# Second mixer: the values of the linear attention are projected ahead of the LRU's gate

## Chip, cores and metric

One core of a Trainium2 chip. The metric is the device time of one execution in microseconds (us); before the change the median of 3 runs is 734.24 us (732.68 to 735.36).

## What is computed

Two transformer blocks in float32 on 256 tokens of width 1024. The change lies in the mixer of the second block, which joins three branches:

```
z = einsum('bsd,de->bse', rms_norm(x, norm_mix), w_in)
a_x, a_y, b_q, b_f, b_i, b_g, c_q, c_k, c_v = split(z)
ya = rglru_group(a_x, a_y, ...)      # h = scan(conv(a_x)); h * gelu(a_y)
yb = hgrn2_group(b_q, b_f, b_i, b_g) # chunked recurrence with values b_i; rms_norm(o) * silu(b_g)
yc = moba_group(c_q, c_k, c_v)       # attention
y = concat([rms_norm(ya), yb, rms_norm(yc)])
x = x + einsum('bse,ed->bsd', y, w_out)
```

`a_y` gates the LRU's scan; `b_i` are the values of the linear attention (the recurrence); `b_g` gates its normed output.

## The kernel before, in words

Weights are streamed. `Weights` holds a list of chunks (1 MB each for this projection, 256 columns of the output); a DMA on SP brings a chunk into one of two `raw` buffers, and each half chunk (a unit) is split into a high part (`whi`, ScalarE, line 130) and the rest (`wlo`, VectorE, line 131). `blocks` takes two units of a chunk one after the other; for each it makes one output block of 128 columns by 256 tokens in PSUM (`mm`): 8 steps of k with 3 products each (`whi` with `ah`, `whi` with `al`, `wlo` with `ah`), 24 products. All products are issued by the helper at line 260, transposes at line 256; small operations go through helpers at lines 214 (two tensors), 233 (scalar, tensor, tensor), 228 and 229 (tensor, scalars), 236 and 239 (ScalarE).

`mixer2` walks over `self.c_in2`, which pairs the names of the table `ORDER2` with the chunks of `w_in_2`; `laid_out` packs that matrix in the table's order, so the table alone says in which order the 12 chunks come. For each block that is ready, `mixer2` does what its name asks: for `a_y` the gelu by tanh, in `gyz` and `gy` (product with `rb`, square, `gy`, tanh, `gy`); for `b_i` a copy `vt`, transposes and a scaling into `hv`; for `b_g` a product `hgz`, a tanh and `hgg`. After the chunk `a_x` the generator `lru` is started, after `b_i` the recurrence `hg` is finished and its tail `hg_out` started, after `c_v` half of the attention's heads (`moba`). Generators are advanced one piece after each block (`bg.step`). A scheduler then lays the instructions of each engine in its order; the engines run their queues in that order and wait on semaphores.

`lru` needs both blocks of `a_y`: after its scans (`xc`, line 1204) it multiplies by `gy`, squares into `lt`, sums the two halves, lets TensorE sum over the partitions (`ones`,`lt`), makes the reciprocal root on VectorE (`ncv`, `ncw`, `ncr`, eight small operations), broadcasts it by TensorE (`ident`,`ncr`), and writes the normed result split into `mab`. `moba` ends in the same norm over its sum of squares `ycs` and writes `mc`. `hg_out` multiplies the recurrence's matrices `attT` and `attX` with `hv`, squares (`hee`), sums per head (`cst`,`hee`), makes its root (`hn`), waits until `b_g` has been gated, and writes the other half of `mab`.

After the loop `bg.finish(lr, *mo)` completes `lru` and `moba`; then the output projection begins with its four first blocks on `lru`'s half of `mab` and on `mc`, and takes the recurrence's half last.

Of the kernel before, what the change touches and what calls it, by code (L numbers as in the profile page):

```python
# [1710 lines left out]
def tile_two_blocks(ctx, tc, I, out, dbg=None, auto=True):  # L1711
    if not auto:
# [2 lines left out]


ORDER2 = (("b_f", 768), ("b_q", 512), ("c_q", 1536), ("c_k", 2048), ("c_v", 2560), ("c_q", 1792),
          ("c_k", 2304), ("c_v", 2816), ("a_x", 0), ("a_y", 256), ("b_i", 1024), ("b_g", 1280))


def _spans(widths):
# [108 lines left out]
```

## Time and profile before

| | us |
|---|---|
| median of 3 runs | 734.24 |
| the profiled execution's own time | 730.46 |
| its span, first to last instruction | 728.7 |
| TensorE busy (products) | 703.0, 96% |
| VectorE busy | 559.0, 77% |
| ScalarE busy | 436.5, 60% |
| mean granted TensorE clock | 0.995 |

A row of the profile gives the line, the engine, the operation, what it writes and from what, and the count. A float32 product appears as two records for one instruction, so a count of 8 can be four instructions. Products overlap, so busy time says little; what counts is when the next one starts.

### The profile page before, as it was taken

To read this page: it belongs to the slowest core of one execution; us is meant where nothing else is said; L and a number is where in the kernel's file an instruction comes from. 1 tells how busy PE (TensorE), PEld (TensorE's weight loads), DVE (VectorE), ACT (ScalarE), POOL (GpSimd) and SP (SyncE) were. 2 spreads that over 40 slices of the span, in tenths; PEclk is the share of its full clock that TensorE was granted. 3 is DMA by queue.
4 is the path that set the end of the run, shared out by engine and by line. 5 is a ranking of instruction groups with operands and counts; after the bars stand their busy time and mean duration, and the time that the engine had idled before them with its cause. 6 is when DMAs were issued, how large, how long until landed. Compare 5 with 4: busy or idle time off the path is not lost.

```text
span 728.7 us, 13820 instructions
## 1 busy us (share of the span) xinstructions
PE 703.0 (96%) x5442; PEld 664.3 (91%) x5442; DVE 559.0 (77%) x1240; ACT 436.5 (60%) x807; POOL 24.3 (3%) x74
## 2 busy tenths in 40 slices
PE   8998998999999999999999998999899999999996
PEld 5887897989999999999999998898799999988895
DVE  8997787987989987887656598997777777744533
ACT  7489558655566655555455486769467666643421
POOL 5020000000001000000000200000000000000000
PEclk9999999999999999999999999999999999999999
DMA  7552303236555655455556545332237665565521
GB/s 256 201 185 107 117 2 116 66 109 207 184 189 203 212 193 175 174 174 181 179 177 215 183 167 174 116 115 69 107 116 239 205 220 176 188 215 177 182 107 58
DMA packets 18225, 117.25 MB, mean 161 GB/s; under 512 B 2160, under 2 KB 2416, under 8 KB 5360
## 3 DMA queue, kind: packets, MB, share of 16 engines
q1 hardware_dynamic: 17136, 113.55, 45.8%
q0 software_dynamic: 448, 2.16, 0.8%
q8 instruction: 43, 0.70, 0.4%
q10 hardware_dynamic: 576, 0.65, 0.3%
q14 instruction: 22, 0.18, 0.1%
HBM read 115.30 MB, written 1.05 MB: 160 GB/s over the span
## 4 chain that ended last, share of the span: by engine, by line
PE 79%; DVE 11%; ACT 6%; DMA 2%; issue 1%; SPq 0%; DVEq 0%; ACTq 0%
PE mm L260 71%; PE ps L260 6%; DVE wlo L131 2%; PE ps L256 1%; ACT whi L130 1%; DVE s5w L214 1%; DMA cst<-in_cst_dram 1%; ACT s5tz L239 1%; DVE s5bc L214 1%; DMA raw<-in_w_up_dram 1%; ACT us L239 1%; DVE s5x L214 1%; PE pso L260 1%; ACT msc L236 1%; DVE s5an L233 1%
## 5 line engine op out<-in xcount | busy, mean ns | idle before, releaser
L130 ACT ACTIVATE whi<-raw 128x1024 fp32r<-128x1024 f32 (+1 forms) x206 | 215.4, 1051 | 200.5 <-PE mm L260 172.7
L131 DVE TENSOR_TENSOR wlo<-raw,whi 128x1024 fp32r<-128x1024 f32 (+1 forms) x206 | 249.8, 1214 | 108.2 <-ACT whi L130 106.8
L260 PE MATMUL mm<-ah,whi 128*128 128x258 f32 (+2 forms) x992 | 281.8, 284 | 0.5 <-DVE a L214 0.5
L260 PE MATMUL mm<-al,whi 128*128 128x258 f32 (+2 forms) x992 | 280.6, 283 | 0.0
L260 PE MATMUL mm<-ah,wlo 128*128 128x258 f32 (+2 forms) x992 | 280.3, 283 | 0.0
L260 PEld LDWEIGHTS mm<-ah,whi 128*128 128x128 f32 x992 | 187.8, 189 | 2.2 <-issue 1.0
L260 PEld LDWEIGHTS mm<-al,whi 128*128 128x128 f32 x992 | 187.8, 189 | 1.8 <-issue 1.1
L260 PEld LDWEIGHTS mm<-ah,wlo 128*128 128x128 f32 x992 | 187.9, 189 | 0.5 <-issue 0.4
L260 PE MATMUL mm<-wlo,f2h 128*128 128x256 f32 (+1 forms) x160 | 55.6, 348 | 0.0
L260 PE MATMUL mm<-whi,f2h 128*128 128x256 f32 (+1 forms) x160 | 55.5, 347 | 0.0
L260 PE MATMUL mm<-whi,f2l 128*128 128x256 f32 (+1 forms) x160 | 55.5, 347 | 0.0
L260 PE MATMUL mm<-fh,whi 128*128 128x256 f32 x176 | 48.6, 276 | 0.0
L260 PE MATMUL mm<-fl,whi 128*128 128x256 f32 x176 | 48.6, 276 | 0.0
L260 PE MATMUL mm<-fh,wlo 128*128 128x256 f32 x176 | 48.6, 276 | 0.0
L260 PEld LDWEIGHTS mm<-whi,f2h 128*128 128x128 f32 x160 | 30.3, 189 | 3.9
L260 PEld LDWEIGHTS mm<-wlo,f2h 128*128 128x128 f32 x160 | 30.3, 189 | 3.8
L260 PEld LDWEIGHTS mm<-whi,f2l 128*128 128x128 f32 x160 | 30.3, 189 | 3.8
L260 PEld LDWEIGHTS mm<-fh,whi 128*128 128x128 f32 x176 | 33.0, 188 | 0.0
L260 PEld LDWEIGHTS mm<-fl,whi 128*128 128x128 f32 x176 | 33.0, 188 | 0.0
L260 PEld LDWEIGHTS mm<-fh,wlo 128*128 128x128 f32 x176 | 33.0, 188 | 0.0
L260 PE MATMUL mm<-hT,whi 128*128 128x272 f32 (+1 forms) x128 | 29.3, 389 | 0.7 <-ACT ah L239 0.7
L260 PEld LDWEIGHTS mm<-hT,whi 128*128 128x128 f32 x128 | 23.8, 190 | 5.9 <-ACT ah L239 1.5
(411 smaller groups left out, 1092.9 us busy)
## 6 DMA issues: line engine op xcount, KB each, us to landing
raw<-in_w_ff_dram SPq DMA_DIRECT2D x32, 1024.0 KB, 4.8
raw<-in_w_in_dram SPq DMA_DIRECT2D x24, 1024.0 KB, 4.8
raw<-in_w_up_dram SPq DMA_DIRECT2D x22, 1024.0 KB, 4.8
raw<-in_w_down_dram SPq DMA_DIRECT2D x8, 1024.0 KB, 4.8
whi<-in_w_in_dram SPq DMA_DIRECT2D x8, 512.0 KB, 5.4
raw<-in_w_o_dram SPq DMA_DIRECT2D x4, 1024.0 KB, 4.7
raw<-in_w_out_dram SPq DMA_DIRECT2D x4, 1024.0 KB, 4.8
raw<-in_w_down_dram SPq DMA_DIRECT2D x4, 768.0 KB, 4.4
```

Of the source, the lines that this page charges most:

```text
L130: b.A.activation(out=hi[:, 0:m], in_=raw, func=AF.Copy)
L131: b.V.tensor_tensor(out=lo[:, 0:m], in0=raw, in1=hi[:, 0:m].bitcast(F32), op=ALU.subtract)
L214: return self.V.tensor_tensor(out=o, in0=a, in1=b, op=op)
L233: return self.V.scalar_tensor_tensor(out=o, in0=a, scalar=s, in1=b, op0=op0, op1=op1)
L236: return self.A.activation(out=o, in_=i, func=f, **k)
L239: return self.A.activation(out=o, in_=i, func=AF.Copy)
L256: return self.PE.transpose(out=o, in_=i, identity=self.ident[0:k, 0:k])
L260: return self.PE.matmul(out=o, lhsT=l, rhs=r, start=start, stop=stop)
```

## The change

Two chunks trade places in the table: `b_i` comes before `a_y`. Nothing else is edited; the packing of the weights follows the table.

```
 ORDER2 = (("b_f", 768), ("b_q", 512), ("c_q", 1536), ("c_k", 2048), ("c_v", 2560), ("c_q", 1792),
-          ("c_k", 2304), ("c_v", 2816), ("a_x", 0), ("a_y", 256), ("b_i", 1024), ("b_g", 1280))
+          ("c_k", 2304), ("c_v", 2816), ("a_x", 0), ("b_i", 1024), ("a_y", 256), ("b_g", 1280))
```

How this moves the instructions is seen at three places. The first is TensorE at the end of the loop, from the last block product of `b_g` to the first product of the output projection. Before:

```order
L260 MATMUL mm<-ah,wlo 128x256
L260 MATMUL ps<-ident,ncr 128x128 x2
L260 MATMUL ps<-attT,hv 64x128 x2
L260 MATMUL ps<-attX,hv 64x128 x2
L260 MATMUL ps<-attT,hv 64x128 x4
L260 MATMUL ps<-attX,hv 64x128 x2
L260 MATMUL ps<-attT,hv 64x128 x2
L260 MATMUL ps<-ones,ycs 128x1 x2
L260 MATMUL mm<-mab,whi 128x256 x4
```

After the change, the same place:

```order
L260 MATMUL mm<-ah,wlo 128x256
L260 MATMUL ps<-ones,lt 128x1 x2
L260 MATMUL ps<-ident,ncr 128x128 x2
L256 MATMUL ps<-ident,hn 4x128 x2
L260 MATMUL ps<-ones,ycs 128x1 x2
L260 MATMUL mm<-mab,whi 128x256 x4
```

And after the change where the blocks of `a_y` end and those of `b_g` begin (its first product is the third row here):

```order
L260 MATMUL pso<-mwt,cvn 64x256 x2
L260 MATMUL pso<-mwt,cvn 64x128 x2
L260 MATMUL mm<-ah,whi 128x256
L260 MATMUL ps<-cst,hee 128x2 x4
L260 MATMUL mm<-al,whi 128x256
L260 MATMUL mm<-ah,wlo 128x256
```

The twelve products with `hv` have left the end (they stand between the two blocks of `a_y`), `cst`,`hee` has moved ahead of `b_g`'s blocks, and `ones`,`lt`, which stood 19 block products before the loop's end, stands behind the last.

The second place is the gelu of `a_y`'s second block, on VectorE and ScalarE. VectorE before, from `gyz` to the last `gy`:

```order
L214 TENSOR_TENSOR gyz<-mm,rb_5197 128x256
L1430 ISA msc,msm<-ps,cst 128x128
L1430 ISA msm 128x1
L1430 ISA msc,msm<-ps,cst 128x256
L1430 ISA msm 128x1
L131 TENSOR_TENSOR wlo<-raw,whi 128x1024
L233 SCALAR_TENSOR_TENSOR gy<-gy,gyz 128x256
L228 TENSOR_SCALAR msm<-msm 128x2
L1445 COPY mwt<-ps 128x384
L233 SCALAR_TENSOR_TENSOR lrd<-lrd,lt 128x512
L233 SCALAR_TENSOR_TENSOR gy<-gy,gyz 128x256
```

VectorE after the change, from the first scan on:

```order
L1204 SCALAR_TENSOR_TENSOR xc<-lrd,lth 128x256
L233 SCALAR_TENSOR_TENSOR gy<-gy,gyz 128x256
L1204 SCALAR_TENSOR_TENSOR xc<-lrd,lth 128x256
L214 TENSOR_TENSOR gyz<-mm,rb_5197 128x256
L229 TENSOR_SCALAR hn<-ps 128x8
L229 TENSOR_SCALAR hn<-hn 128x8
L214 TENSOR_TENSOR hn<-hn 128x8
L233 SCALAR_TENSOR_TENSOR hn<-hn 128x8 x2
L131 TENSOR_TENSOR wlo<-raw,whi 128x1024
L233 SCALAR_TENSOR_TENSOR gy<-gy,gyz 128x256
L214 TENSOR_TENSOR hn<-hn 128x8
L131 TENSOR_TENSOR wlo<-raw,whi 128x1024
```

ScalarE there after the change, from the exchange of its table of functions to the second tanh:

```order
L236 ACT_TABLE_LOAD
L236 ACTIVATE gy<-gy 128x256
L236 ACTIVATE hee<-ps 128x512
L239 ACTIVATE hls<-ps 128x512
L130 ACTIVATE whi<-raw 128x1024
L236 ACTIVATE gy<-gyz 128x256
L130 ACTIVATE whi<-raw 128x1024
L239 ACTIVATE yc<-pso 128x256
L130 ACTIVATE whi<-raw 128x1024
L236 ACTIVATE gy<-gy 128x256
```

The last `gy` stood six operations ahead of the scans; now the second block's begins behind both scans, with the splits of two units in its way on either engine.

The third place is VectorE from the last `gy` to the norm `ncv` of the LRU. Before, from the scans on:

```order
L1204 SCALAR_TENSOR_TENSOR xc<-lrd,lth 128x256 x2
L1445 COPY mwt<-ps 128x384
L131 TENSOR_TENSOR wlo<-raw,whi 128x1024
L214 TENSOR_TENSOR xc<-xc,gy 128x512
L131 TENSOR_TENSOR wlo<-raw,whi 128x1024
L214 TENSOR_TENSOR lt<-lt 128x256
L214 TENSOR_TENSOR hgz<-mm,rb_5197 128x256
L229 TENSOR_SCALAR ncv<-ps 128x2
```

After the change, from the last `gy` on:

```order
L233 SCALAR_TENSOR_TENSOR gy<-gy,gyz 128x256
L233 SCALAR_TENSOR_TENSOR hn<-hn 128x8
L214 TENSOR_TENSOR ycs<-ycs,sqc 128x256
L214 TENSOR_TENSOR xc<-xc,gy 128x512
L233 SCALAR_TENSOR_TENSOR hgg<-hgg,hgz 128x256
L131 TENSOR_TENSOR wlo<-raw,whi 128x1024
L214 TENSOR_TENSOR lt<-lt 128x256
L214 TENSOR_TENSOR hgz<-mm,rb_5197 128x256
L229 TENSOR_SCALAR ncv<-ps 128x2
```

Before, the product of `xc` with `gy` followed the scans; now it follows the last `gy`.

## Rows read from the trace of the kernel before

**Rows 1.** The page: busy time by engine, and the chain that ended last.

```profile
PE 703.0 (96%) x5442; PEld 664.3 (91%) x5442; DVE 559.0 (77%) x1240; ACT 436.5 (60%) x807; POOL 24.3 (3%) x74
...
PE 79%; DVE 11%; ACT 6%; DMA 2%; issue 1%; SPq 0%; DVEq 0%; ACTq 0%
```

**Rows 2.** Busy time by stretch: length, engines, granted clock, DMA share, GB/s.

```profile
512.00:521.00 9.00, 6.35 (x62) 5.80 (x62) 7.01 (x28) 4.24 (x10) 0.00 (x0) 0.97 0.38 129
521.00:535.00 14.00, 13.98 (x106) 13.61 (x107) 8.67 (x25) 6.82 (x14) 0.00 (x0) 0.89 0.00 1
```

**Rows 3.** TensorE's waits, 412 to 570 us: total us, times, longest.

```profile
PE ps L260 <- DVE ncr L233: 1.4, 2, 0.9
PE mm L260 <- ACT mc L239: 1.4, 1, 1.4
```

**Rows 4.** The chain that ended last, in order of time: start, us, what.

```profile
421.48 15.72 PE mm L260 x136
...
511.87 1.07 ACT whi L130
```

**Rows 5.** Timeline, gelu of the second block of `a_y`: start, us, engine, line, operation.

```profile
494.74 0.43 DVE L214 TENSOR_TENSOR gyz<-mm,rb 128x256 f32<-128x256 f32 x1 [1.03 <-PE mm L260]
...
496.03 0.41 ACT L236 ACTIVATE gy<-gyz 128x256 f32<-128x256 f32 x1
...
498.04 0.41 ACT L236 ACTIVATE gy<-gy 128x256 f32<-128x256 f32 x1
...
498.79 0.42 DVE L233 SCALAR_TENSOR_TENSOR gy<-gy,gyz 128x256 f32<-128x256 f32 x1
```

**Rows 6.** Timeline, the LRU branch from its scans to the output projection.

```profile
503.57 1.27 DVE L1204 TENSOR_TENSOR_SCAN xc<-lrd,lth 128x256 f32<-128x256 f32 x2
...
506.35 0.68 DVE L214 TENSOR_TENSOR xc<-xc,gy 128x512 f32<-128x512 f32 x1
...
509.64 0.16 DVE L229 TENSOR_SCALAR ncv<-ps 128x2 f32<-128x2 f32 x1 [0.48 <-PE ps L260]
...
512.88 0.71 PE L260 MATMUL ps<-ident,ncr 128*128 128x128 f32 x4 [0.93 <-DVE ncr L233]
```

**Rows 7.** Timeline of TensorE, the small products around the loop's end.

```profile
505.35 0.86 PE L260 MATMUL pso<-mwt,cvn 128*64 128x256 f32 x6
...
509.10 0.50 PE L260 MATMUL ps<-ones,lt 128*128 128x1 f32 x4
...
513.52 0.44 PE L260 MATMUL ps<-attT,hv 128*64 128x128 f32 x4
...
514.98 0.61 PE L260 MATMUL ps<-ones,ycs 128*128 128x1 f32 x4
515.45 0.72 PE L260 MATMUL mm<-mab,whi 128*128 128x256 f32 x4
...
517.48 0.28 PE L260 MATMUL mm<-mab,wlo 128*128 128x256 f32 x1
518.19 0.68 PE L260 MATMUL ps<-ident,ncr 128*128 128x128 f32 x4 [0.43 <-DVE ncr L233]
518.71 0.95 PE L260 MATMUL ps<-cst,hee 128*128 128x2 f32 x8
521.02 1.22 PE L260 MATMUL mm<-mc,whi 128*128 128x256 f32 x4 [1.36 <-ACT mc L239]
```

**Rows 8.** Busy time in two single microseconds behind the holes (columns as rows 2).

```profile
522.00:523.00 1.00, 1.00 (x7) 1.00 (x6) 1.00 (x5) 0.53 (x2) 0.00 (x0) 0.50 0.00 0
524.00:525.00 1.00, 1.00 (x9) 0.80 (x8) 0.00 (x0) 0.37 (x1) 0.00 (x0) 1.00 0.06 16
```

**Rows 9.** Timeline of ScalarE, the exchange of its table of functions.

```profile
499.62 1.28 ACT L236 ACT_TABLE_LOAD   x1
...
500.91 0.63 ACT L236 ACTIVATE lth<-lt 128x512 f32<-128x512 f32 x1
```

## The prediction

> **What bounds the kernel now.** I read the page first. TensorE is busy for 96% of the span and holds 79% of the chain that ended last, so a change elsewhere pays only where TensorE stands still [rows 1]. Next come the stretches around the edit: from 512 to 521 us TensorE is busy for 6.35 of 9 us, and from 521 to 535 us it is busy throughout but at a mean granted clock of 0.89 [rows 2]. TensorE's waits between 412 and 570 us name what it stood for: twice the reciprocal root `ncr` of a norm (1.4 us in all), and once the split normed attention output `mc` (1.4 us) [rows 3]. With the issue gaps around them these are three holes: 511.8 to 512.88, 517.6 to 518.19, and 519.66 to 521.02 us [rows 4, 7]. The end of the first is the LRU branch's norm, that of the other two the attention's. Until 511.8 us TensorE runs block products almost without a hole (the first weight slot of the last chunk comes free at 511.87 us); 136 of them took 15.72 us, so one costs 0.116 us, and a chunk of 48 costs 5.5 us [rows 4].
>
> **What the change removes and adds.** Nothing: the same blocks, the same DMAs, the same count of instructions. Two chunks trade places in the stream; the weights are packed in the same table's order, so SP's and POOL's queues are unchanged. Only the order on TensorE, VectorE and ScalarE moves.
>
> **What comes earlier.** The values `b_i` are ready one chunk sooner, so the recurrence's 12 output products (`attT`, `attX`, from 513.52 to 514.98, 1.46 us [rows 7]) and the four `cst`,`hee` products of its norm (0.95 us [rows 7]) now run before the last chunk `b_g`, where before they stood behind it. That is 2.4 us of TensorE work taken out from behind the last chunk. In return `ones`,`lt` (0.50 us [rows 7]) moves from the middle of that chunk to behind it. The last block therefore ends near 511.8 + 1.46 + 0.95 - 0.50 = 513.7 us.
>
> **What comes later.** The gate chunk `a_y` is now the last but one. Its end, counted back from 513.7 us: 48 block products of `b_g` (5.5 us), `hee` (0.95) and the last `pso` group (0.86, [rows 7]) come after it, so its second block ends near 506.4 us. From there one chain runs over VectorE and ScalarE to TensorE:
> 1. The order puts the second `gyz` behind the second scan on VectorE; two scans took 1.27 us [rows 6], one is 0.6. Bounds 0 and 1.3 us; I take 0.6, one scan: `gyz` at 507.0.
> 2. The gate itself. Before, the second block took from 494.74 to 499.21 us, 4.5 us [rows 5], of which the four operations are 1.7 and the rest queueing. Now two `whi` and a `yc` stand on ScalarE between square and tanh, and two `wlo` with four small `hn` operations on VectorE. Bounds 4.5 (as before) and 5.5 (one more `whi`, 1.07 us [rows 4]); I take 5.0: 512.0 us.
> 3. One `ycs` addition stands ahead of `xc`x`gy`: 0.3 us. Then `xc`x`gy` to the norm's first operation `ncv`, 506.35 to 509.64 before, 3.3 us [rows 6]: 515.6 us. There is one `wlo` in that piece now and two before, but `hgg` and a `whi` have joined, so I keep 3.3.
> 4. `ncv` to the product with `ncr`, 509.64 to 512.88 before, 3.2 us [rows 6], again with a `wlo` and three short operations between: 518.8 us.
>
> Before, the same product started at 512.88 us and TensorE had waited 1.1 us for it. Now it starts 5.9 us later; TensorE has been out of block products since 513.7 us and waits some 4.6 us, with only `ones`,`lt` between. What is queued behind it on TensorE is every output projection.
>
> **Behind that product.** The 2.4 us of recurrence work is already done: -2.4. But it was also the cover of the next wait: from the `ncr` product to the first `mab` product passed 2.57 us (512.88 to 515.45 [rows 6, 7]), filled with these products. Now `ncr`, two transposes and `ones`,`ycs` fill about 1.3 of them: +1.3. The attention's norm, formerly bare (0.6 and 1.4 us [rows 3, 7]), now has the `mab` products and the gated recurrence beside it; I give back 1.6 of these 2.0 us, bounds 1.1 and 2.0.
>
> **Clock.** At 522 to 523 us the clock is 0.50, the 1.2 GHz level, after TensorE had been idle for 1.4 us and thinly used before; at 524 to 525 us it is full again [rows 8]. Seven products in that microsecond against nine in the later one, over about 3 us from 521 us on, cost at least 0.7 us; by the block's 0.116 us doubled, 1.5 us. The new wait is longer, so I expect the fall to come earlier and to cost about the same: 0, bounds -1.5 (no fall) and +1.5 (a second one).
>
> **Sum.** +5.9 - 2.4 + 1.3 - 1.6 + 0 = **+3.2 us**. The profiled execution took 730.46 us, 0.5% under the median of 734.24; the sum is a difference inside one stage, so I put it on the median: 737.4 us (733.7 on that execution). Low ends together (0, 4.5, gain 2.0, clock -1.5): about 0; high ends (1.3, 5.5, gain 1.1, clock +1.5): about +6.5.
>
> **Rivals.**
> - *Covered chain, no change* (0.20): the gate chain runs nearer to its four operations' 1.7 us than to 4.5, say 3.0 us, since the tail has VectorE less full. Then the shift is 3.9 instead of 5.9 and the sum +1.2: 735.4 us. Against: VectorE was busy 7.01 of 9 us there [rows 2], with wide splits in order.
> - *The recurrence's tail was what held the end* (0.07), faster: if the LRU norm's product came no later than 514.8 us, as close behind the last block as before (1.1 us), the shift would be 1.9 instead of 5.9, all of the attention's 2.0 us of waits would go and the half clock's 1.5 with them: +1.9 - 2.4 + 1.3 - 2.0 - 1.5 = -2.7, 731.5 us. It decides at `gy` ready by 514.8 - 3.2 - 3.3 - 0.3 = 508.0 us, 1.6 us after its block's end; the four operations alone take 1.7 [rows 5].
> - *The reload lands on the chain* (0.04): the square root's table of functions is loaded at 499.62 us [rows 9] and exchanged back later; the change moves that exchange ahead of the first block's tanh, and VectorE holds the first block's last `gy` between the two scans, with the second block's `gyz` behind them. Where the exchange ends last there, its 1.29 us (499.62 to 500.91 [rows 9]) come on top: 738.7 us. Against: the first block has 2.8 us of block products as a lead. The Trainium skill (ScalarE: Activation LUTs, What ACT_TABLE_LOAD costs) gives 1.28 us for the load and a drain of about 1.38 besides; by it this case would be 740.1 us. The trace disagrees about the drain: the next operation starts 0.01 us after the load's end.
> - *The clock falls and stays* (0.06): the wait before `ncr` is followed by thin work and a second wait. If a second stretch at 1.2 GHz follows, block products at twice 0.116 us lose another 1.5 us: 738.9 us, and 740.2 with the exchange. For it: the half clock followed a shorter hole [rows 8]. The Trainium skill (TensorE: Matmul & The Clock Gate, What's actually happening) lets the clock go by how busy TensorE has lately been; the trace agrees with one fall here, and no row of before shows two.
>
> **How the numbers follow.** My forecast, a bare LRU chain, has 0.63. 0.3% of 734.24 is 2.2 us, about what a measurement of this kernel can tell from no change: the band is 732.0 to 736.4. The forecast, the exchange and the clock lie above it but for the forecast's low tail (0.04), which with the covered chain makes 0.24; faster is 0.07, slower 0.69. The range goes from 734.6, inside the covered case, to 740.2, the end of the clock case.
>
> **What would show it.** Right: TensorE's longest wait of the second mixer is on `ncr`, 3 to 5 us, right behind the last block products; `xc`x`gy` starts some 6 us later than 506.35; the waits on `mc` shrink below 0.5 us; everything before `a_x` is the same. Wrong: `xc`x`gy` within 2 us of its old time, or TensorE's wait on `ncr` staying near 1 us, or a new wait ahead of the recurrence's output products.

## The result and the profile after

| | before | after |
|---|---|---|
| median of 17 runs, us | 731.76 | 736.75 |
| lowest to highest, us | 728.97 to 735.36 | 734.63 to 739.70 |
| the profiled execution's own time, us | 730.46 | 734.94 |
| its span, us | 728.7 | 733.2 |
| mean granted TensorE clock | 0.995 | 0.992 |

The changed kernel is slower: ratio 1.0068, 95% interval 1.0053 to 1.0083, which is 5.0 us. The trace after is of a run on the quick side: its 734.94 us is the second lowest of the 17, and its mean granted clock the highest of them (their median is 0.988). The page, against [rows 1]: the busy times are the same but for the clock, and in the chain that ended last VectorE has 13% where it had 11.

```profile
PE 705.3 (96%) x5442; PEld 667.0 (91%) x5442; DVE 559.0 (76%) x1240; ACT 436.6 (60%) x807; POOL 24.2 (3%) x74
...
PE 78%; DVE 13%; ACT 6%; issue 2%; DMA 1%; SPq 0%; DVEq 0%
```

The same two stretches as [rows 2], then four single microseconds against [rows 8] (columns as in rows 2):

```profile
512.00:521.00 9.00, 3.10 (x17) 2.62 (x15) 6.01 (x19) 2.75 (x5) 0.00 (x0) 0.73 0.57 208
521.00:535.00 14.00, 13.23 (x91) 13.05 (x92) 7.42 (x25) 4.12 (x10) 0.00 (x0) 0.81 0.02 8
...
515.00:516.00 1.00, 0.00 (x0) 0.00 (x0) 1.00 (x6) 0.00 (x1) 0.00 (x0) 1.00 0.00 0
516.00:517.00 1.00, 0.00 (x0) 0.00 (x0) 1.00 (x2) 0.00 (x0) 0.00 (x0) 0.57 0.00 0
...
526.00:527.00 1.00, 1.00 (x8) 0.92 (x7) 0.56 (x2) 0.49 (x2) 0.00 (x0) 0.81 0.00 0
527.00:528.00 1.00, 1.00 (x9) 0.99 (x9) 1.00 (x4) 0.96 (x3) 0.00 (x0) 1.00 0.00 0
```

From 512 to 521 us TensorE is busy for 3.10 us where it was 6.35. The clock falls to its 1.2 GHz level within 516 to 517 us, while TensorE is idle, and is full again within 526 to 527 us; the nine microseconds between read 0.50. A mean of 0.57 is 0.86 us at half clock and 0.81 is 0.38, so the stretch lasts 0.86 + 9 + 0.38 = 10.24 us. The single microseconds of before give 3.41 in the same way, from 520.5 us on.

TensorE's waits from 412 to 575 us, against [rows 3] (total us, times, longest):

```profile
PE ps L260 <- DVE ncr L233: 3.5, 1, 3.5
PE ps L260 <- DVE lt L214: 2.1, 1, 2.1
PE ps L260 <- DVE qzs L228: 1.7, 1, 1.7
...
PE mm L260 <- ACT mab L239: 1.1, 1, 1.1
```

The wait on the attention's scaled queries `qzs` lies far ahead of the edit and is no part of the loss: it was there before, 1.8 us, the longest wait of the window, though [rows 3] don't show it. Both waits on the attention's norm are gone, `mc` and the second `ncr`. In their place TensorE waits 2.1 us for `lt`, the input of the LRU norm, 3.5 us for that norm, and 1.1 us for the first `mab`. The rows answering to [rows 6, 7], in order of time:

```profile
506.16 0.40 DVE L214 TENSOR_TENSOR gyz<-mm,rb 128x256 f32<-128x256 f32 x1
...
511.62 0.69 DVE L214 TENSOR_TENSOR xc<-xc,gy 128x512 f32<-128x512 f32 x1
...
514.98 0.16 DVE L229 TENSOR_SCALAR ncv<-ps 128x2 f32<-128x2 f32 x1 [0.42 <-PE ps L260]
...
518.41 1.19 PE L260 MATMUL ps<-ident,ncr 128*128 128x128 f32 x4 [3.47 <-DVE ncr L233]
```

The chain that ended last, from the second gate block to the norm's product (start, us, what), in place of TensorE's block products:

```profile
507.74 1.22 DVE wlo L131
508.96 0.33 DVE gy L233
509.29 0.08 DVE hn L214
509.37 1.13 DVE wlo L131
510.50 0.07 DVE hn L233
510.58 0.34 DVE hgz L214
510.92 0.38 DVE gy L233
...
512.64 1.14 DVE wlo L131
513.79 0.44 DVE lt L214
...
516.01 1.14 DVE wlo L131
...
518.10 0.17 DVE ncr L233
518.28 0.14 issue
518.41 1.19 PE ps L260 x4
```

Of the 12.25 us from `gyz` (506.16) to the product (518.41), four `wlo` hold 1.22 + 1.13 + 1.14 + 1.14 = 4.63. None of them belongs to the LRU branch. They split weights of the mixer's output projection and stand in VectorE's queue between the chain's own steps. Ahead of the first line shown, the chain comes from TensorE's `cst`,`hee` through five small `hn` operations, which also stand in that queue, behind `gyz`.

**Where the 5 us lie.** The second mixer's stage can be measured within one execution, from the first `ident`,`msc` product after 480 us to the last `mc`,`wlo` product. After:

```profile
484.02 0.33 PE L256 MATMUL ps<-ident,msc 128*128 128x128 f32 x1 [0.35 <-ACT msc L236]
...
547.73 0.28 PE L260 MATMUL mm<-mc,wlo 128*128 128x256 f32 x1
```

That is 63.71 us. Before, the same two products start at 485.04 and 543.32: 58.28 us. The stage is 5.43 us longer. TensorE's holes in it are the waits with the issue gaps: 2.27 + 3.63 + 1.27 = 7.17 us after, 1.10 + 0.60 + 1.53 = 3.23 us before, a difference of 3.94. The clock: after, TensorE was idle for 2.27 us (516.14 to 518.41) and 1.27 us of the 10.24, so 6.7 us of work ran at half speed, which cost half of that, 3.35 us. Before, 2.9 us of work ran so, from 521.02 us to the end of the stretch near 523.94, and cost 1.46. That is 1.9 us more. Holes and clock together make 5.8 us against the 5.43 measured.

That the two come so close is partly chance, for one thing more differs. At full clock, and with TensorE busy throughout, the products near the stage's end start 0.1178 us apart after and 0.1133 us before. Ten microseconds of each, after first (columns as in [rows 2]):

```profile
536.00:546.00 10.00, 10.00 (x87) 10.00 (x87) 10.00 (x20) 6.88 (x14) 0.00 (x0) 1.00 0.34 111
532.00:542.00 10.00, 10.00 (x91) 10.00 (x90) 10.00 (x20) 6.98 (x15) 0.00 (x0) 1.00 0.31 107
```

Over the 21 us from the clock's return to the stage's end that is another 0.8 us (an estimate: 21 x 0.0045 / 0.1178), so the rest of the stage must have been quicker after; that was not taken apart. The two profiled executions as a whole differ by 4.5 us, since the one after reached the stage 1.02 us earlier.

### The profile page after: what moved, and what is told of

It reads as the page before. It is cut to its first block, busy times and chain, and to the rows that moved or that the text cites. A ratio compares the mean times of both kernels' runs of the same rounds, so it can differ in the third digit from the quotient of the medians.

```text
span 733.2 us, 13820 instructions
## 1 busy us (share of the span) xinstructions
PE 705.3 (96%) x5442; PEld 667.0 (91%) x5442; DVE 559.0 (76%) x1240; ACT 436.6 (60%) x807; POOL 24.2 (3%) x74
## 4 chain that ended last, share of the span: by engine, by line
PE 78%; DVE 13%; ACT 6%; issue 2%; DMA 1%; SPq 0%; DVEq 0%
PE mm L260 69%; PE ps L260 7%; DVE wlo L131 3%; PE ps L256 1%; DVE s5w L214 1%; ACT s5tz L239 1%; DMA cst<-in_cst_dram 1%; DVE s5bc L214 1%; ACT whi L130 1%; ACT us L239 1%; DVE s5x L214 1%; PE pso L260 1%; DVE s5an L233 1%; ACT u L239 1%; DVE qzs L214 0%
## 6 DMA issues: line engine op xcount, KB each, us to landing
whi<-in_w_in_dram SPq DMA_DIRECT2D x8, 512.0 KB, 5.6
```

## The experiments

Three theories were to be told apart. **A**: the gate chunk comes late, and the chain behind it has its own length. **B**: VectorE's in-order queue stretches that chain with other work, the `wlo` splits above all. **C**: a part of the loss is not waiting but the clock, which the longer holes pull down for longer. All ratios are to the kernel before. "Stage" is measured as above, in the profiled execution; "norm" is the time from the same first product to the one that waits for the LRU branch's `ncr`, taken from the trace. Each is read from one execution of its kernel, the ratio from 6 to 17.

| kernel | ratio (95%) | stage | norm | half clock in the stage |
|---|---|---|---|---|
| before | 1 | 58.28 | 27.84 | 3.41 |
| after | 1.0068 (1.0053 to 1.0083) | 63.71 | 34.39 | 10.24 |
| e1 after, no gelu | 0.9996 (0.9976 to 1.0016) | 60.78 | 31.93 | 6.83 |
| e2 before, no gelu | 0.9995 (0.9966 to 1.0023) | 56.99 | 26.96 | none |
| e3 after, no LRU norm | 0.9956 (0.9934 to 0.9977) | 57.21 | - | 3.41 |
| e4 after, late tail | 1.0082 (1.0053 to 1.0111) | 65.47 | 32.22 | 10.24 |
| e5 after, filled | 1.0030 (1.0010 to 1.0050) | 61.80 | 34.39 | 3.41 |
| e6 before, filled | 0.9986 (0.9970 to 1.0002) | 57.25 | 27.84 | none |
| e7 after, splits on GpSimd | 1.0094 (1.0074 to 1.0114) | 65.72 | 37.14 | 13.65 |
| e8 before, no LRU norm | 0.9985 (0.9969 to 1.0001) | 57.37 | - | 3.41 |
| e9 after, four splits out | 1.0026 (1.0006 to 1.0046) | 59.86 | 31.36 | 6.83 |
| e10 before, four splits out | 1.0003 (0.9983 to 1.0023) | 58.41 | 25.52 | 3.41 |
| e11 before, keys first, filled | 0.9974 (0.9958 to 0.9990) | 57.29 | 27.88 | none |

A difference of two ratios has the root of the summed squares of their half-widths as its own: about 0.0025, or 1.8 us, against the changed kernel.

**e1, e2: the gate's gelu left out, in the changed kernel and in the one before.**

```
-                        self.mul(z, o, rb)
-                        self.act(g, z, AF.Square, scale=math.sqrt(0.044715))
-                        self.stt(g, g, 1.0, z, ALU.add, ALU.mult)
-                        self.act(g, g, AF.Tanh, scale=math.sqrt(2.0 / math.pi))
-                        self.stt(g, g, 1.0, z, ALU.add, ALU.mult)
+                        self.mul(g, o, rb)
```

> The changed kernel with a_y's gelu left out: gy is a_y's block times rb alone, one VectorE operation instead of five on two engines (that part of the computation is missing). The changed kernel's TensorE has three holes here: 2.1 us ahead of ones,lt, 3.5 us ahead of ident,ncr, 1.1 us ahead of mab. Theory A (the late gate alone): the gate takes 4.7 us less (506.16 to 511.29 us in the trace of the changed kernel), xc x gy starts near 507 us, the norm is done before the block products end, and both of the first holes go, the fall of the clock with them: 5 us or more under the changed kernel, level with before. Theory B (a crowded VectorE): the norm's eight small operations, which stand among the recurrence's, b_g's and the splits', are now spread as long as TensorE's block products last; the hole ahead of ones,lt goes, that ahead of ident,ncr stays near 3 us: 2 to 3 us under the changed kernel.

> The kernel before with the same gelu left out (that part of the computation is missing). The control for the run above: in its trace the gate was ready at 499.2 us and the scans at 504.8, so the gelu had over 5 us of slack. Theories A and B both expect no change, within 0.5 us of before; more than 1 us under it would mean that the gelu costs something by itself (VectorE and ScalarE time), and the run above would have to be read less that.

Without its gelu the changed kernel is level with before, 0.0072 x 732 = 5.3 us (give or take 1.8) faster than with it; the kernel before gains nothing that can be measured. So the gate is on the path that sets the end after the change and was not before. The stage of its traced execution is only 2.93 us shorter (63.71 to 60.78); why the times show more stays open. And the chain got shorter by only 34.39 - 31.93 = 2.46 us, though the gate itself had taken 5.13 us (506.16 to 511.29). The waits show what is left:

```profile
PE ps L260 <- DVE ncr L233: 3.2, 1, 3.2
...
PE mm L260 <- ACT mab L239: 1.1, 1, 1.1
```

The wait on `lt` went, that on `ncr` stayed at 3.2 us: from the norm's first operation `ncv` to the product pass 5.4 us (515.74 to 521.14), where the changed kernel took 3.4. A alone doesn't explain that.

**e3, e8: the LRU branch's norm left out** (an earlier norm's multiplier in its place), in the changed kernel and in the one before.

```
-        self.act(t, xc, AF.Square)
-        self.add(t[:, 0], t[:, 0], t[:, 1])
-        _, rb = self.norm_bc(t[:, 0], SPANS2, 1.0 / 256, "rba", "rba", c)
+        rb = self.rb2
...
+            self.rb2 = rb
```

> The changed kernel with the LRU branch's norm left out (square, sum, ones,lt, the eight small operations, ident,ncr and rba are missing; rb of the layer's norm stands in its place). Theory A and my prediction's sum: the holes of 2.1 and 3.5 us go, the attention's norm comes next as the last to end, with the 0.6 and 1.4 us that it had before or somewhat more: 3 to 5 us under the changed kernel. A rival, that the earlier recurrence itself holds the end (its hn, its broadcast), expects no gain.

> The kernel before with the LRU branch's norm left out (the multiplier of an earlier norm is used instead), the control of the changed kernel without it, which took 0.9956 of the time before. If the whole loss of the change lies in when that norm ends, and the change gives back the recurrence's 2.4 us otherwise, this kernel gains only the norm's own waits, 0.8 to 1.5 us (ratio 0.998 to 0.999), and lies 1.5 to 2.5 us above the changed kernel without the norm. Rival (leaving the norm out is worth about 3 us whatever the order, and the swap is worth nothing without it): ratio 0.996, level with the changed kernel without it.

The norm is worth 0.0112 x 732 = 8.2 us in the changed kernel and 1.1 us (give or take 1.2) in the one before: the whole loss hangs on when this norm ends. What the swap is worth without it stays open. By the times e3 is 0.0029 under e8 (2.1 us, give or take 2.0); by the stages the two are level, 57.21 and 57.37 us, and the waits of e3 say why there need not be a gain: four waits, 2.8 us together, with the recurrence's 2.4 us gone from behind the last chunk, against two of 2.9 us in e8 (`ncr` 1.5, `mc` 1.4).

```profile
PE mm L260 <- ACT mab L239: 1.0, 1, 1.0
...
PE mm L260 <- DVE mab L214: 0.9, 1, 0.9
PE ps L260 <- DVE ncr L233: 0.6, 1, 0.6
PE mm L260 <- ACT mc L239: 0.3, 1, 0.3
```

**e4: the recurrence's output tail starts only behind the last chunk**, as in the kernel before.

```
+                if n == "b_g":
                     ho = bg.add(self.hg_out(), A_HO)
```

> Half of the change alone: the changed kernel's order of chunks, but the recurrence's tail hg_out is started only after b_g, as late as before. If the earlier products of the recurrence (2.4 us of TensorE work taken out from behind the last chunk) pay in the changed kernel, undoing them costs up to 2.4 us less the 1.1 us wait ahead of mab that they would cover: +1.3 us, 738 us. Theory B expects a gain against that, since hn and hls then leave the LRU norm's stretch on VectorE: between -1 and 0 us.

1.0 us over the changed kernel, give or take 2.4: it tells nothing by its time. Its trace has the norm's product 2.17 us earlier (32.22 against 34.39), but that is not B's doing: the second `gyz` already comes 1.95 us earlier (20.19 us into the stage against 22.14), and from there to the product pass 12.03 us where it was 12.25. The small operations of the tail, then, hardly stretch the chain; the four `wlo` are still in it. The stage is longer all the same, with a wait of 0.5 us on the tail's `hls` that the changed kernel hasn't; the rest of that difference was not taken apart.

**e5: products that nothing reads, put into the changed kernel's holes.** Four of them read `xc` behind `xc` x `gy`, seven read `lt` behind `ones`,`lt`.

```
         self.mul(xc, xc, self.gy)
+        idle = self.ps()
+        for _ in range(4):
+            self.mm(idle[:, 0:S], xc[:, 0, 0:P], xc[:, 0])
...
+        self.fill = 7
         _, rb = self.norm_bc(t[:, 0], SPANS2, 1.0 / 256, "rba", "rba", c)
...
             self.mm(p[0:b - a, i:i + 1], acc[:, a:b], self.ones[:, 0:1])
+        if self.fill:
+            idle = self.ps()
+            for _ in range(self.fill):
+                self.mm(idle[:, 0:S], acc[:, 0:P], acc[:, 0:S])
+            self.fill = 0
```

> The changed kernel with products that nothing reads put into TensorE's two holes ahead of the LRU branch's norm (4 products of xc behind xc x gy, 7 of lt behind ones,lt); nothing else is changed and no wait of the chain is shorter. Theory C (a part of the loss is the clock: the changed kernel's half-clock stretch of 10.24 us against 3.41 us before costs some 1.9 us of the 5): the stretch shrinks to 3.41 us or goes, and the time falls by 1.5 to 3 us against the changed kernel, to a ratio of 1.003 to 1.005 to the kernel before. Rival (the loss is the LRU chain's late end alone, and the clock costs nothing that VectorE's chain would not cost anyway): no gain, or up to 0.5 us slower for the products in the way, ratio 1.007.

This is the cleanest of the runs. The norm's product comes at 34.39 us, to the hundredth where it came without the filling, so the chain is no shorter. One useful group moved with the filling: `cst`,`hee` now stands behind the last block; at the norm's product the same work is done in both kernels. What differs behind it is above all the clock:

```profile
512.00:521.00 9.00, 7.66 (x45) 6.58 (x44) 6.77 (x28) 2.76 (x6) 0.00 (x0) 1.00 0.46 168
521.00:535.00 14.00, 13.68 (x99) 13.27 (x100) 7.54 (x26) 4.79 (x11) 0.00 (x0) 0.88 0.08 33
```

The half-clock stretch is 3.41 us instead of 10.24, and the kernel gains 0.0038 x 732 = 2.8 us (give or take 1.8); the stage is 1.91 us shorter. Reckoned as above, 3.35 - 1.7 = 1.65 us of that are the clock; the products near the end of this stage also come 0.1134 us apart, as before the change, so the stage alone can't price the clock to a few tenths. That it is the clock, and not a chance of one execution, is borne out by all runs: the mean granted clock has a median of 0.988 in the 17 runs after the change (0.985 to 0.992), of 0.994 in the 12 here (0.992 to 0.998), and of 0.993 in the kernel before, run beside these, as on two other chips. C holds.

**e6: the same in the kernel before,** three products in the hole ahead of `mc`.

```
         _, rb = self.norm_bc(self.ycs, SPANS2, 1.0 / 512, "rbc", "rba", c)
+        idle = self.ps()
+        for _ in range(3):
+            self.mm(idle[:, 0:S], self.ycs[:, 0:P], self.ycs)
```

> The kernel before with 3 products that nothing reads (of ycs, behind the broadcast of the attention's norm) in TensorE's hole of 1.4 us ahead of mc. Theory C: the half-clock stretch of 3.41 us at 520.5 us goes, and with it about 1.4 us: ratio 0.998, and a kernel that beats both. Rival (the hole and not the clock is what costs): no change, ratio 1.000, or up to 0.3 us slower.

The clock stays full through the stage, the same two stretches:

```profile
512.00:521.00 9.00, 7.63 (x70) 6.81 (x68) 7.38 (x27) 4.74 (x12) 0.00 (x0) 1.00 0.47 160
521.00:535.00 14.00, 13.87 (x115) 13.26 (x116) 9.37 (x28) 7.10 (x16) 0.00 (x0) 1.00 0.00 0
```

The stage is 1.03 us shorter, less than the 1.4 expected, and the time by its ratio 1.0 us lower, at the edge of what the runs can tell (0.9970 to 1.0002).

**e7: four `wlo` of the last projection on GpSimd** (its first four units).

```
-                b.V.tensor_tensor(out=lo[:, 0:m], in0=raw, ...
+                (b.G if u in b.pool_units else b.V).tensor_tensor(out=lo[:, 0:m], in0=raw, ...
...
         self.c_out2 = flat("w_out_2")
+        self.pool_units = [u for ci in self.c_out2 for u in ci][0:4]
```

> The changed kernel with the wlo subtractions of the last projection's first four units on GpSimd, so that they no longer stand in VectorE's in-order queue between the steps of the gate and of the LRU branch's norm. Theory B (the chain is stretched by other work queued on VectorE between its steps): the four subtractions, of some 0.4 us each, leave the chain, the ncr product comes 1 to 1.5 us earlier, and the time falls by 1 to 1.5 us against the changed kernel, ratio 1.005. Theory A (the late start of the gate alone, each step bound by its own engine's latency): no change, ratio 1.007. If the slower engine delivers wlo late, the first output products wait for it and the time rises.

A miss of either theory, for a reason that neither had: 1.9 us slower than the changed kernel (give or take 1.8), the norm's product 2.75 us later. Two splits on GpSimd, 4.73 us together, fell on the gate, and VectorE's 8-element operations stood until they ended:

```profile
507.11 0.17 DVE L229 TENSOR_SCALAR hn<-ps 128x8 f32<-128x8 f32 x1 [0.29 <-PE ps L260]
507.23 4.73 POOL L131 TENSOR_TENSOR wlo<-raw,whi 128x1024 fp32r<-128x1024 f32 x2 [7.34 <-ACT whi L130]
507.31 2.33 DVE L229 TENSOR_SCALAR hn<-hn 128x8 int32<-128x8 int32 x1
509.68 2.31 DVE L214 TENSOR_TENSOR hn<-hn 128x8 f32<-128x8 f32 x1
```

Each took 0.17 us in the changed kernel. (The expectation's 0.4 us for a split was wrong too: VectorE takes 1.13 to 1.22.) So e7 says nothing on B, and e9 takes the splits out without a substitute.

**e9, e10: no `wlo` for the four units that stand in the chain** (the third to the sixth of the last projection); e10 does the same in the kernel before.

```
-            lo = pool.tile([P, 1024], F32R, name="wlo", tag="wlo")
+            lo = hi if u in b.high_only else pool.tile([P, 1024], F32R, name="wlo", tag="wlo")
...
+                if lo is not hi:
+                    b.V.tensor_tensor(out=lo[:, 0:m], in0=raw, ...
...
+        self.high_only = [u for ci in self.c_out2 for u in ci][2:6]
```

> The changed kernel without the wlo subtractions of the four units of the last projection (the third to the sixth) that stand in VectorE's queue between the second gyz and the last step of the LRU norm's ncr; their products use whi in wlo's place, so the low part of these weights is left out. Unlike on GpSimd, nothing takes their place. Theory B (the in-order VectorE queue stretches the chain): about 3 us of the 4 x 1.13 us come off the chain, the ncr product starts about 3 us earlier, the two waits of 2.1 and 3.5 us shrink together to about 2.7, the half-clock stretch gets shorter, and the time falls by 3 to 5 us against the changed kernel: ratio 1.000 to 1.003. Theory A (only the gate's late start and each operation's own latency count): less than 1 us, ratio 1.006.

> The control: the kernel before without the same four wlo subtractions (the low part of these weights is left out). Theory B: here the same splits stretch a chain that is late by 1.1 us only, so 0.5 to 1.5 us: ratio 0.998 to 0.9995. If the splits cost the same in both orders (rival: a general saving of VectorE work, not of the moved chain), the gain is the 3 to 5 us of the changed kernel, ratio 0.994.

In the changed kernel the product comes 34.39 - 31.36 = 3.03 us earlier and the time falls by 0.0042 x 732 = 3.1 us (give or take 1.8). All of the 3.03 us lie in the chain: the second `gyz` stands 22.14 us into the stage in both, and from it to the product pass 9.22 us instead of 12.25. In the kernel before, the product moves by 2.3 us and the time by nothing that can be measured (1.0003, give or take 1.5 us): there its chain was 1.1 us late, and of the hole that went the next one gave a part back (0.84 us where 0.60 had been). Its stage is not shorter either (58.41 against 58.28), but there the products near the end come 0.1178 us apart in place of 0.1133, some 0.7 us of it. So B holds, and pays only where the chain is bare. e9's waits:

```profile
PE ps L261 <- DVE ncr L234: 2.5, 1, 2.5
...
PE mm L261 <- ACT mab L240: 1.1, 1, 1.1
```

The wait on `lt` is gone and that on `ncr` 1.0 us shorter; the half-clock stretch is 6.83 us, so a part of the 3.1 us is clock. Of e10's own expectation, 0.5 to 1.5 us, nothing was seen; the interval excludes its upper end.

**e11: a version to beat both**: the order of before, but the attention's first key chunk ahead of its first query chunk, with the filling of e6.

```
-ORDER2 = (("b_f", 768), ("b_q", 512), ("c_q", 1536), ("c_k", 2048), ("c_v", 2560), ...
+ORDER2 = (("b_f", 768), ("b_q", 512), ("c_k", 2048), ("c_q", 1536), ("c_v", 2560), ...
```

> A version meant to beat both: the order of before with the attention's first key chunk ahead of its first query chunk, and the 3 products that nothing reads behind the broadcast of the attention's norm. The filled kernel before alone took 0.9986 of the time before. If the chunk order saves the 0.6 us that the trace's durations give for it, the ratio is 0.997 to 0.998; if not, 0.9986; a loss above 1.000 would mean that the exchange opens a new wait ahead of the attention's scores.

Ratio 0.9974 (0.9958 to 0.9990): 1.9 us under the kernel before and some 7 under the changed one, the fastest of the kernels here that leave out no part of the computation. As in e6 the wait on `mc` is gone and the clock stays full through the stage. TensorE's wait on the attention's scaled queries `qzs` is 0.9 us, 1.8 in before and 1.7 in e6:

```profile
PE ps L260 <- DVE ncr L233: 1.4, 2, 0.9
PE ps L260 <- DVE qzs L228: 0.9, 1, 0.9
```

That the chunk order brings the difference to e6 is not shown: 0.0012 lies inside either interval, and e5 and e10, with the order of before there, waited for `qzs` for 1.1 us too.

## Why the prediction was right and where it was not

The sign and the mechanism were right, and the time is inside the range, 0.65 us under the forecast. That closeness is partly luck: the sum was put on a median of 734.24 us from three runs, and 17 runs gave 731.76. The predicted difference was +3.2 us and the measured one +5.0.

The stage began 1.02 us earlier in the profiled execution after, so its times are shifted by that much here.

| step | predicted | measured |
|---|---|---|
| second `gyz` | 507.0 | 507.2 |
| end of the gate | 512.0, 5.0 us long | 512.3, 5.1 us long |
| `ncv` | 515.6 | 516.0 |
| product with `ncr` | 518.8 | 519.4 |
| end of the last block | 513.7 | 513.1 |
| wait behind it, without `ones`,`lt` | 4.6 us | 2.10 + 3.47 = 5.6 us |
| wait ahead of `mab` | 1.3 us | 1.1 us |
| attention's waits given back | 1.6 of 2.0 us | all |
| clock | 0 | +1.9 us |

- **The chain's steps** held to 0.2 or 0.3 us each, all on the same side. They were sized by rows of before in which the same interleaving with `wlo` already stood, so B was inside the durations, named only as queueing. (Step 3 counts two `wlo` before between `xc`x`gy` and `ncv`; there is one, as after, and the piece took 3.36 us.) e9 shows that 3 us of the chain are those splits.
- **The holes**: predicted 5.9 - 2.4 + 1.3 - 1.6 = +3.2, measured +3.94. The product came 0.6 us later and the blocks ended 0.6 us earlier than forecast; the attention's norm gave back all of its waits.
- **The clock is the step that failed**: "I expect the fall to come earlier and to cost about the same: 0". It came earlier, while TensorE stood still for the second of three holes, and stayed three times as long, past the upper bound of +1.5. The rival "the clock falls and stays" priced it nearly rightly (1.5 us) with a different picture, a second stretch behind the first, and had 0.06. e5, which changes the clock and leaves the norm's product where it was, is the run that shows it.
- **The rivals.** The covered chain (+1.2) fell: the gate took 5.1 us, and from the second `gyz` to `xc`x`gy` VectorE was busy for 5.04 of 5.46 us. The tail as what held the end, needing `gy` by 508.0 us, missed by over four. Both rivals set the gate's own work at four operations and 1.7 us; it has five, 2.1 us, for the first `gy` (497.31 us before, 0.42 us) is not among [rows 5]. The table exchange was not on the chain: it lies at 503.25 us, the tanh behind it at 504.54, and the `gy` that waits for it starts right where the first scan ends.

```profile
503.25 1.28 ACT L236 ACT_TABLE_LOAD   x1
504.54 0.42 ACT L236 ACTIVATE gy<-gy 128x256 f32<-128x256 f32 x1
```

As before ([rows 9]), the next operation starts 0.01 us behind the load, and the one before it ended 0.02 us ahead: this trace, too, shows none of the drain that the Trainium skill gives (ScalarE: Activation LUTs, What ACT_TABLE_LOAD costs).

- **"What would show it"** came true but in one point: the longest wait is on `ncr`, 3.5 us, `xc` x `gy` is 6.3 us later than 506.35 with the shift, and `mc` is no longer waited for. The hole, though, is split over two waits, and `lt` has the first.

## What to carry to other kernels

Before a chunk is moved ahead of another, follow what the one behind feeds: a branch of many small dependent operations, in order on an engine with wide splits in between, takes longer than its own steps (here splits were 4.63 of 12.25 us), and it became bare when its chunk came last but one. Price a new hole on TensorE at more than its length, because the clock can fall in it and the work behind it then runs at half speed for a while; filling it with products that nothing reads shows how much of a loss is clock, if the mean clock of all the runs rises with it. And measure a stage between two fixed instructions of the same execution, which leaves out what differs elsewhere; but it is one execution, and the spacing of its products alone moved a stage by up to 0.8 us here.

## What was not expected of the hardware

- **The half clock outlasts its cause.** After the change the last hole ended at 521.77 us, and the clock was back only within 526 to 527 us, although TensorE worked throughout from there. By and large the longer stretch went with the longer holes: 3.2 us of holes and 3.41 us at half clock in before, 7.2 and 10.24 in after, 8.8 and 13.65 in e7; but e2, with 3.1 us of holes, kept the full clock.
- **The same hole doesn't always bring the clock down.** Near 61 to 64 us TensorE waits 2.3 us in every kernel here. In the profiled executions of before, after and e7 the clock stays full there; in the other ten it falls. Before and e6, 62 to 64 us:

```profile
62.00:64.00 2.00, 0.28 (x3) 0.31 (x4) 1.01 (x3) 1.95 (x6) 0.00 (x0) 1.00 0.00 0
```

```profile
62.00:64.00 2.00, 0.29 (x2) 0.32 (x3) 1.02 (x3) 1.95 (x6) 0.00 (x0) 0.84 0.00 0
```

What decides it stays open. The clock goes with a part of the 6 us by which runs of one kernel differ: of 85 runs of the kernel before, the 27 with a mean granted clock of 0.995 or more took 730.8 us on average, the 29 with 0.991 or less 733.8.

- **Products have two spacings at full clock.** The same products of 256 columns start 0.1133 or 0.1178 us apart, for tens of microseconds on end. The instructions alone don't decide it: e8's edit touches only the LRU branch, long after 400 us, and yet e8 is slower there than the kernel before. The kernel before first, then e8 (columns as in [rows 2]):

```profile
380.00:400.00 20.00, 20.00 (x179) 20.00 (x178) 13.07 (x19) 11.01 (x17) 0.00 (x0) 1.00 0.55 181
380.00:400.00 20.00, 20.00 (x172) 20.00 (x172) 11.45 (x16) 10.03 (x14) 0.00 (x0) 1.00 0.51 168
```

From 360 to 414 us e1, e8 and e10 have the wider spacing, the other ten the narrower one. Whether it goes by the execution or by the kernel is not shown, with one trace of each, nor what sets it; it costs 0.8 us in 20.

- **GpSimd stops VectorE.** In e7, VectorE's operations between buffers of SBUF took 2.33 and 2.31 us instead of 0.17 and ended with GpSimd's, while the one before them, which reads PSUM, took its usual 0.17. The Trainium skill (SBUF — State Buffer, SBUF: two separate sides) has the two engines share a pair of ports that one of them holds for a whole instruction; the trace agrees, also for operations of 8 elements. And the split itself takes 4.73 / 2 = 2.4 us on GpSimd where VectorE takes 1.22.
